# Feed-forward weight tiles split into two parts by GpSimd's casting and adding transfers

## The chip, the cores and the metric

The kernel runs on one core of a Trainium2 chip, as one launch. The metric is the device time of one execution in microseconds (us). A core has TensorE (matrix products, PE in the profile, with its weight loads as PEld), VectorE (DVE), ScalarE (ACT), GpSimd (POOL) and SyncE (SP, which here only issues transfers). Each engine works through its own queue in order, and waits on semaphores for the others.

## The reference

One layer of a diffusion backbone: 512 latent tokens and 256 context tokens, model width 1024, batch 1, all in float32. After the token mixers (a state-space scan and windowed attention) comes the part that matters here:

```python
def conv_ffn(h, w_up, conv_w, conv_b, w_down):
    u = dwconv_centred(h @ w_up, conv_w, conv_b)
    a, b = u[..., :D_FF], u[..., D_FF:]          # D_FF = 2816
    return (jax.nn.silu(a) * b) @ w_down
...
x = x + gt2 * conv_ffn(modulate(x, norm2_g[l], sh2, sc2), w_up[l], ffn_conv_w[l], ffn_conv_b[l], w_down[l])
...
return rmsnorm(x, final_g)
```

`sh2`, `sc2` and `gt2` are parts of `mod`, the product of the activated condition vector with `w_mod`.

## The kernel before

**Products in three passes.** TensorE multiplies in a shortened float format (float32r). To keep float32 accuracy every operand is split in two: `hi` is the value rounded to float32r, `lo` what is left over. A product is then hi x hi, hi x lo and lo x hi, accumulated in one PSUM bank. `gemm` (lines 190 to 201) does this for one weight tile: for each block of 128 x 128 weights, line 196 multiplies the weights' hi with the activations' hi, 197 with their lo, 199 the weights' lo with the activations' hi. So a tile's `lo` is first needed by its third matmul.

**Weight tiles.** A tile has 128 partitions by 1024 columns, eight blocks (512 KB). `load_raw` (143) has SP load it in float32 into a tile `wraw`, of which there are three buffers; `split` (151) has ScalarE write `hi` (a rounding copy, line 152) and VectorE write `lo` (a subtraction, line 153). `whi` and `wlo` have two buffers each, so two tiles are in use or being made, and up to three more lie in raw form. The same raw buffers carry the modulation weights: a key `("m", i)` is loaded and used raw, by VectorE's products with the condition vector in `m_step` (lines 739 to 759; 750, 752, 758 in the profile). `ELSEWHERE` gives a few tiles another place: `("up", 1)` goes to a corner of the feed-forward's result tiles `fh` and `fl` (`far_piece`, line 1851) that is not yet written.

**The order of work.** `run` (170) takes a list of steps, each with the keys of the tiles that it uses, and loads tiles in that order, a fixed number ahead of use. The instructions go through a scheduler that sets each engine's order; each engine then runs its own queue in order.

**The feed-forward stages.** `out_last` (1783) ends the output projection in two halves of 256 tokens, and starts the normalisation: sums of squares (line 239, TensorE), `ms` (249, VectorE), the inverse root `rs` (250, GpSimd), and a spread over partitions (256, TensorE). `norm2_k` (1812) makes the normalised activations `mh` and `ml`, block by block: `tb` (1815, VectorE), `mh` (1816, ScalarE), and `ml` by VectorE (1822) or, for odd blocks, GpSimd (1820). The first up step interleaves this with its products (1866). Steps 1 to 21 each use two tiles, `("up", t)` and `("up", 22 + t)`; between the products ScalarE and VectorE do the three-tap convolution, the gate, and the split of the result (1844 to 1849, and 1347 to 1349 for the first half). The remaining eight `m` steps are woven between the up steps. Then `down_step` (1894) makes seven output blocks from three tiles each (1024, 1024 and 768 columns), and `down_last` (1905) the eighth, the final normalisation and the stores. `close_c1` (1824) opens the pool `c2pool`, which holds `fh` and `fl`.

Of the kernel before, what the change touches and what calls it, by code (L numbers as in the profile page):

```python
# [10 lines left out]
F32R = mybir.dt.float32r  # L11
U8 = mybir.dt.uint8
AF = mybir.ActivationFunctionType
ALU = mybir.AluOpType
# [4 lines left out]
P = 128  # L19
# [5 lines left out]
NFF = 22  # L25
# [14 lines left out]
def raw(ap):  # L40
    return ap.bitcast(F32)
# [3 lines left out]
def tile_hybrid_layer(  # L45
# [31 lines left out]
    V, S, G, T = nc.vector, nc.scalar, nc.gpsimd, nc.tensor  # L77

    cpool = ctx.enter_context(tc.tile_pool(name="cpool", bufs=1))
    wpool = ctx.enter_context(tc.tile_pool(name="wpool", bufs=2))  # L80
# [37 lines left out]
    src = {}  # L118
# [24 lines left out]
    def load_raw(key):  # L143
        a, n = src[key]
        r = wpool.tile([P, 1024], F32, tag="raw", name="wraw", bufs=3)
        dma = nc.sync.dma_start(r[:, :n], a)
        if key[0] == "m":
            M_LOADS[key[1]] = dma
        return r, n

    def split(r, n, hi, lo):
        S.copy(hi[:, :n], r[:, :n])  # L152
        V.tensor_tensor(lo[:, :n], r[:, :n], raw(hi[:, :n]), ALU.subtract)  # L153

    ELSEWHERE = {}

    def load(key):
        r, n = load_raw(key)
        if key[0] == "m":
            return r  # L160
        if key in ELSEWHERE:
            hi, lo = ELSEWHERE[key]()
            split(r, n, hi, lo)
            return hi, lo
        hi = wpool.tile([P, 1024], F32R, tag="whi", name="whi", bufs=2)
        lo = wpool.tile([P, 1024], F32R, tag="wlo", name="wlo", bufs=2)
        split(r, n, hi, lo)
        return hi, lo

    def run(prog, early=None):  # L170

        seq = [k for keys, _ in prog for k in keys]
        have, nload, nuse = {}, 0, 0
        for keys, fn in prog:
            nuse += len(keys)
            while nload < min(nuse + 1 + (early in keys), len(seq)):
                have[seq[nload]] = load(seq[nload])
                nload += 1
            fn(*[have.pop(k) for k in keys])
# [102 lines left out]
    class Plan:  # L282
# [6 lines left out]
        def add(self, name, engine, cost, needs, rank, emit, whole=True, load=0.11, late=False):  # L289


            self.atoms[name] = dict(
                name=name, engine=engine, cost=cost, needs=needs, rank=rank, emit=emit, whole=whole, load=load,
                late=late, start=None,
            )
# [537 lines left out]
    Q, F = {}, {}  # L833
# [48 lines left out]
    q_split(first["q"], 0)  # L882
    k_step(0)[1](first["w"], first["r"])
    run([q_step(1), ([("v", i) for i in range(3)], v_step)])

    psum_pools(acc=(2, 1), score=(1, 2), pt=(3, 1), po=(1, 1))
# [724 lines left out]
    for g in range(4):  # L1611
# [6 lines left out]
        for c in range(4):  # L1618
# [4 lines left out]
            if c == 1 or g == 3:  # L1623
                prog += m[1 + c : 2 + c] if g == 3 else m[1:2]
        prog += s[9:10]
    run(prog)
    bpool.close()

# [44 lines left out]

    ELSEWHERE["os", 2] = lambda: tuple(yh[3][:, i : i + 2, :].rearrange("p a b -> p (a b)") for i in (0, 2))

# [82 lines left out]
    def piece_in(tag):  # L1758
        def fn():
            t = cp.tile([P, 2, 1024], F32R, tag=tag, name="wlast")  # L1760
            return t[:, 0, :], t[:, 1, :]

        return fn


    for o in (5, 6, 7):
        ELSEWHERE["out", o] = piece_in("yh%d" % (o - 5))

# [55 lines left out]
    def close_c1():  # L1824
        c1pool.close()
        c2pool = ctx.enter_context(tc.tile_pool(name="c2pool", bufs=1, reuse_waits="tile"))
        F["h"] = c2pool.tile([P, NFF, L], F32R, name="fh")
        F["l"] = c2pool.tile([P, NFF, L], F32R, name="fl")

# [24 lines left out]

    ELSEWHERE["up", 1] = far_piece

# [48 lines left out]
    def down_last(*w):  # L1905
# [52 lines left out]
        with tc.manual_schedule(engines={mybir.EngineType.PE}):  # L1958
# [6 lines left out]
            for f in (r["f"], finish(1)):  # L1965
                for _ in f:
                    pass

    run(
        [([], lambda: (y_split(range(8)), [square(True) for _ in range(4)], y_split(range(8, 12))))]  # L1970
        + fill[n3:]
# [3 lines left out]
        + weave([out_step(o) for o in range(5)], msteps[18:24])  # L1975
        + [([], vectors)]
        + [([("out", o) for o in (5, 6, 7)], out_last), ([], close_c1)]
        + weave([up_step(t) for t in range(NFF)], msteps[24:])
        + [down_step(o) for o in range(7)]
        + [([("dn", 21 + i) for i in range(3)], down_last)],  # L1980
        early=("g", 15),
# [85 lines left out]
```

## Time and profile before

| | |
|---|---|
| median of 2 runs | 1241.22 us (1241.05 and 1241.39) |
| span of the profiled execution, first to last instruction | 1239.5 us |
| TensorE busy | 1230.0 us, 99% |
| VectorE busy | 864.6 us, 70% |
| ScalarE busy | 656.3 us, 53% |
| GpSimd busy | 145.4 us, 12% |
| moved by transfers | 174.57 MB, 141 GB/s on average |

The page comes from one execution. Its own time is that of the span and the 1.6 to 1.9 us around it in the two runs. Engine rows give busy time and share of the span; matmuls overlap one another, so their durations add up to more than their pace. In a group, the name before the arrow is the tile that is written, the number after the bar the total busy time and the mean of one in ns, and the last field the idle time before and what ended it. A chain of waits goes back from the last instruction to what released each step. "To landing" is the time from the issue of a transfer to its completion.

### The profile page before, as it was taken

To read this page: it belongs to the slowest core of one execution; us is meant where nothing else is said; L and a number is where in the kernel's file an instruction comes from. 1 tells how busy PE (TensorE), PEld (TensorE's weight loads), DVE (VectorE), ACT (ScalarE), POOL (GpSimd) and SP (SyncE) were. 2 spreads that over 40 slices of the span, in tenths; PEclk is the share of its full clock that TensorE was granted. 3 is DMA by queue.
4 is the path that set the end of the run, shared out by engine and by line. 5 is a ranking of instruction groups with operands and counts; after the bars stand their busy time and mean duration, and the time that the engine had idled before them with its cause. 6 is when DMAs were issued, how large, how long until landed. Compare 5 with 4: busy or idle time off the path is not lost.

```text
span 1239.5 us, 17395 instructions
## 1 busy us (share of the span) xinstructions
PE 1230.0 (99%) x6464; PEld 1013.8 (82%) x6464; DVE 864.6 (70%) x1387; ACT 656.3 (53%) x1224; POOL 145.4 (12%) x145
## 2 busy tenths in 40 slices
PE   9999999999999999999999999999999999999997
PEld 6798888888888878777787788889888888888886
DVE  5857788888645697896987767576777767772333
ACT  5658788787454476475675653224544444442221
POOL 0000000000000052261542530000100000000000
PEclk9999999999999999999999999999999999999999
DMA  9643142222354336355365577674233333333331
GB/s 371 248 136 94 56 137 81 91 72 77 119 173 132 127 102 184 115 157 158 102 187 203 146 257 262 213 231 159 89 117 119 109 113 119 112 106 97 103 94 68
DMA packets 91189, 174.57 MB, mean 141 GB/s; under 512 B 7904, under 2 KB 43552, under 8 KB 91104
## 3 DMA queue, kind: packets, MB, share of 16 engines
q1 hardware_dynamic: 90128, 172.66, 43.9%
q8 instruction: 51, 0.84, 0.3%
q10 hardware_dynamic: 976, 0.79, 0.2%
q14 instruction: 34, 0.28, 0.1%
HBM read 150.82 MB, written 17.11 MB: 135 GB/s over the span
## 4 chain that ended last, share of the span: by engine, by line
PE 93%; DMA 3%; DVE 3%; ACT 1%; issue 0%; POOL 0%; DVEq 0%; SPq 0%; ACTq 0%; POOLq 0%
PE acc L196 21%; PE acc L199 21%; PE acc L197 21%; PE score L914 3%; PE po L963 3%; PE pt L950 2%; PE mis L536 2%; PE mis L1567 2%; PE mis L1460 2%; PE mis L1575 1%; DMA wraw<-wout 1%; PE acc L1033 1%; PE acc L1034 1%; PE acc L1035 1%; PE mis L1477 1%; PE mis L1375 1%
## 5 line engine op out<-in xcount | busy, mean ns | idle before, releaser
L153 DVE TENSOR_TENSOR wlo<-wraw,whi 128x1024 fp32r<-128x1024 f32 (+2 forms) x127 | 156.0, 1228 | 125.9 <-ACT whi L152 123.0
L152 ACT CAST whi<-wraw 128x1024 fp32r<-128x1024 f32 (+2 forms) x127 | 131.2, 1034 | 196.3 <-PE acc L197 142.5
L196 PE MATMUL acc<-hlh,whi 128*128 128x512 f32 x472 | 194.2, 411 | 0.0
L197 PE MATMUL acc<-hll,whi 128*128 128x512 f32 x472 | 185.0, 392 | 0.0
L199 PE MATMUL acc<-hlh,wlo 128*128 128x512 f32 x472 | 185.0, 392 | 0.0
L196 PE MATMUL acc<-mh,whi 128*128 128x512 f32 x368 | 143.4, 390 | 0.0
L197 PE MATMUL acc<-ml,whi 128*128 128x512 f32 x368 | 143.2, 389 | 0.0
L199 PE MATMUL acc<-mh,wlo 128*128 128x512 f32 x368 | 143.2, 389 | 0.0
L199 PEld LDWEIGHTS acc<-hlh,wlo 128*128 128x128 f32 x472 | 88.6, 188 | 19.5
L196 PEld LDWEIGHTS acc<-hlh,whi 128*128 128x128 f32 x472 | 88.8, 188 | 17.9 <-issue 3.1
L197 PEld LDWEIGHTS acc<-hll,whi 128*128 128x128 f32 x472 | 88.9, 188 | 17.4 <-issue 2.4
L1462 POOL TENSOR_TENSOR st<-st,eT 128x512 f32<-128x512 f32 x24 | 29.5, 1230 | 448.7 <-ACT st L1479 435.0
L197 PEld LDWEIGHTS acc<-ml,whi 128*128 128x128 f32 x368 | 69.1, 188 | 14.4
L196 PEld LDWEIGHTS acc<-mh,whi 128*128 128x128 f32 x368 | 69.1, 188 | 14.3
L199 PEld LDWEIGHTS acc<-mh,wlo 128*128 128x128 f32 x368 | 69.1, 188 | 14.2
L1348 DVE SCALAR_TENSOR_TENSOR ta<-acc,half,ta 128x511 f32<-128x511 f32 (+1 forms) x66 | 43.9, 665 | 27.3 <-ACT ta L1347 27.1
L923 DVE CUSTOM_DVE_ANT_0 p<-score,winm,nsink 128x512 f32<-128x512 f32 (+1 forms) x64 | 51.8, 810 | 15.3 <-PE score L914 13.8
L250 POOL TENSOR_TENSOR rs<-ms,phalf 128x2 f32<-128x2 f32 (+1 forms) x5 | 4.8, 956 | 475.2 <-DVE ms L249 475.2
L196 PE MATMUL acc<-fh,whi 128*128 128x512 f32 x154 | 60.0, 390 | 0.0
L197 PE MATMUL acc<-fl,whi 128*128 128x512 f32 x154 | 59.9, 389 | 0.0
L199 PE MATMUL acc<-fh,wlo 128*128 128x512 f32 x154 | 59.9, 389 | 0.0
L1347 ACT ACTIVATE ta<-acc,half 128x512 f32<-128x512 f32 (+1 forms) x66 | 46.9, 711 | 22.5 <-PE acc L199 21.2
(381 smaller groups left out, 2891.4 us busy)
## 6 DMA issues: line engine op xcount, KB each, us to landing
wraw<-wup SPq DMA_DIRECT2D x44, 512.0 KB, 3.4
fb<-cs_d SPq DMA_DIRECT2D x32, 512.0 KB, 6.2
wraw<-wm SPq DMA_DIRECT2D x32, 512.0 KB, 3.6
wraw<-wx SPq DMA_DIRECT2D x24, 512.0 KB, 3.6
wm<-wm SPq DMA_DIRECT2D x16, 512.0 KB, 8.4
wraw<-wz SPq DMA_DIRECT2D x16, 512.0 KB, 3.5
wraw<-wos SPq DMA_DIRECT2D x16, 512.0 KB, 4.8
wraw<-wdn SPq DMA_DIRECT2D x16, 512.0 KB, 3.5
```

What stands on the lines that cost most here:

```text
L152: S.copy(hi[:, :n], r[:, :n])
L153: V.tensor_tensor(lo[:, :n], r[:, :n], raw(hi[:, :n]), ALU.subtract)
L196: T.matmul(ps, wh, xh[:, k0 + k, :], start=a, stop=False)
L197: T.matmul(ps, wh, xl[:, k0 + k, :], start=False, stop=False)
L199: T.matmul(ps, wl, xh[:, k0 + k, :], start=False, stop=b)
L536: T.matmul(ps, w[a], h[b], start=c == 1, stop=c % n == 0, skip_group_check=True)
L914: T.matmul(ps[:, o : o + len(z) * P], Q[h][:, b * P : (b + 1) * P], k[:, j, z[0] * P : (z[-1] + 1) * P], start=v == 0 and o % 512 in (0, P ...
L923: V.tensor_tensor_reduce(p[:, :w], d["ps"][i][:, o0 : o0 + w], m, op0=ALU.add, op1=ALU.min, scale=1.0, scalar=nsink[:, h : h + 1], accum_o ...
L963: T.matmul(d["po"], vst[:, cols[x], j, :], d[y][x], start=x == 0 and y == "pth", stop=x == c - 1 and y == "ptl")
L1347: S.activation(o[:, :n], ps[:, :n], AF.Identity, scale=hcol(base_w, stride + i), bias=hcol(base_b, i))
L1348: V.scalar_tensor_tensor(o[:, 1:n], ps[:, 0 : n - 1], hcol(base_w, i), o[:, 1:n], ALU.mult, ALU.add)
L1462: G.tensor_tensor(h8(n), h8(s), bc64(eT[:, z0 : z0 + 8, c]), ALU.mult)
```

## The change

In place of load, rounding copy and subtraction, each tile of `w_up` and `w_down` except the first three used (`("up", 0)`, `("up", 22)`, `("up", 1)`) is made by a new function `load_split`: GpSimd issues a transfer from memory that casts into `hi`; ScalarE writes the negative of `hi` into `lo`; GpSimd issues a second transfer of the same weights that adds them into `lo`. No raw buffer is used. Two tiles of three use the buffers `whi` and `wlo`, the third a new pair `xhi` and `xlo` in `c2pool`, with one buffer each. In these stages tiles are asked for one further ahead.

```diff
+    THIRD = []
+
+    def load_split(key):
+
+        a, n = src[key]
+        THIRD.append(key)
+        if len(THIRD) % 3:
+            hi, lo = (wpool.tile([P, 1024], F32R, tag=t, name=t, bufs=2) for t in ("whi", "wlo"))
+        else:
+            hi, lo = (F["c2"].tile([P, 1024], F32R, tag=t, name=t, bufs=1) for t in ("xhi", "xlo"))
+        G.dma_start(hi[:, :n], a)
+        S.activation(lo[:, :n], raw(hi[:, :n]), AF.Copy, scale=-1.0)
+        G.dma_start(lo[:, :n], a, accum_op=ALU.add)
+        return hi, lo
 
     def load(key):
+        if key[0] in ("up", "dn") and key not in (("up", 0), ("up", 1), ("up", NFF)):
+            return load_split(key)
         r, n = load_raw(key)
...
         for keys, fn in prog:
             nuse += len(keys)
-            while nload < min(nuse + 1 + (early in keys), len(seq)):
+            more = keys and keys[0][0] in ("up", "dn")
+            while nload < min(nuse + 1 + (early in keys) + bool(more), len(seq)):
                 have[seq[nload]] = load(seq[nload])
...
         c2pool = ctx.enter_context(tc.tile_pool(name="c2pool", bufs=1, reuse_waits="tile"))
+        F["c2"] = c2pool
         F["h"] = c2pool.tile([P, NFF, L], F32R, name="fh")
```

## The prediction

> **What bounds the kernel now.** I read the page first: engine totals, slices and the chain that ended last.
>
> ```profile
> span 1239.5 us, 17395 instructions
> PE   1230.0 (99%) x6464; PEld 1013.8 (82%) x6464; DVE 864.6 (70%) x1387; ACT 656.3 (53%) x1224; POOL 145.4 (12%) x145
> PEclk9999999999999999999999999999999999999999
> PE 93%; DMA 3%; DVE 3%; ACT 1%; issue 0%; POOL 0%; DVEq 0%; SPq 0%; ACTq 0%; POOLq 0%
> ```
>
> TensorE holds the chain. That is an average, so next comes the view of busy time by stretches, cut at the feed-forward stages: the first up step with its normalisation, the other up steps, the down products, the tail.
>
> ```profile
> core 0: us, PE busy (x) PEld busy (x) DVE busy (x) ACT busy (x) POOL busy (x), PEclk, DMA share, GB/s
> 866.00:878.40 12.40, 12.40 (x102) 12.02 (x102) 7.89 (x17) 7.74 (x18) 5.92 (x7) 1.00 0.14 44
> 878.40:1112.00 233.60, 233.60 (x1036) 193.46 (x1036) 170.09 (x216) 101.75 (x131) 0.00 (x0) 1.00 0.35 113
> 1112.00:1228.00 116.00, 116.00 (x574) 98.58 (x573) 35.01 (x38) 27.43 (x33) 0.70 (x1) 1.00 0.27 81
> 1228.00:1239.50 11.50, 3.51 (x27) 2.98 (x26) 6.33 (x17) 0.88 (x3) 2.11 (x3) 0.78 0.52 182
> ```
>
> From 878.4 to 1228 TensorE is never idle. Matmul durations overlap (389 ns each below), so I take the pace from the chain in order of time: three matmuls, one weight block, from one L197 to the next.
>
> ```profile
> 882.15 0.23 PE acc L197
> 882.83 0.23 PE acc L197
> ```
>
> That is 0.68 us a block, 0.227 a matmul: **5.44 us for a tile of eight blocks**, 4.08 for the 768-wide tiles of the down product. The groups by line of 880 to 1120 us show what the split costs other engines, and beside it the modulation products:
>
> ```profile
> L196 PE MATMUL acc<-mh,whi 128*128 128x512 f32 x328 | 127.7, 389 | 0.0
> L153 DVE TENSOR_TENSOR wlo<-wraw,whi 128x1024 fp32r<-128x1024 f32 x44 | 53.9, 1224 | 34.5 <-ACT whi L152 34.5
> L152 ACT CAST whi<-wraw 128x1024 fp32r<-128x1024 f32 x44 | 46.3, 1055 | 27.2 <-PE acc L197 27.2
> L1848 ACT CAST fh<-ta 128x512 fp32r<-128x512 f32 x22 | 13.7, 621 | 59.3 <-DVE ta L1847 59.3
> L752 DVE SCALAR_TENSOR_TENSOR tm<-wraw,csil,tm 128x512 f32<-128x512 f32 x14 | 10.5, 747 | 0.4 <-DMA wraw<-wm 0.2
> L758 DVE TENSOR_REDUCE mod<-mis 128x4 f32<-128x512 f32 x2 | 1.4, 692 | 1.8 <-PE mis L756 1.8
> L750 DVE TENSOR_SCALAR tm<-wraw,csil 128x512 f32<-128x512 f32 x2 | 1.0, 480 | 0.1
> ```
>
> **What the change removes is worth nothing.** The two programs' orders of instructions show 65 tiles changed (the short description says 63): 41 of wup, 24 of wdn. VectorE loses 65 subtractions, about 65 x 1.224 = 80 us; ScalarE swaps a cast for a negating copy of the same size, 1.05 us; SP loses 65 loads. No TensorE idle time stands against any of these between 878.4 and 1228, so I credit 0; the cover is TensorE itself, which has no gap to give back.
>
> **What it adds is a serial chain on one queue.** GpSimd now issues 130 transfers. Before, a raw tile waited in its own buffer and only cast and subtraction (2.3 us) followed once an operand buffer was free. Now the load itself goes into that buffer, so it starts only when TensorE has finished the tile there; then come negation, the second transfer, and only then the tile's third matmul (0.45 us in). In the up steps GpSimd's order repeats by three (tiles counted from the first changed one):
>
> ```
> xhi 6 (after TensorE ends 3)  wlo 5  xlo 6  whi 7  wlo 7  whi 8  xhi 9 (after TensorE ends 6)  wlo 8 ...
> ```
>
> Each `lo` waits for ScalarE, and everything behind it waits too: whi 8 cannot be issued until wlo 7 has been, though its buffer is free. This is the wait that I expect last.
>
> No transfer of this sort is in the trace. The nearest rows are SP's plain transfers of the same 512 KB, the spread of the weight loads (last line, issue to landing), and GpSimd's shortest and longest instruction nearby:
>
> ```profile
> wraw<-wup SPq DMA_DIRECT2D x44, 512.0 KB, 3.4
> fb<-cs_d SPq DMA_DIRECT2D x32, 512.0 KB, 6.2
> wraw<-wm SPq DMA_DIRECT2D x32, 512.0 KB, 3.6
> wm<-wm SPq DMA_DIRECT2D x16, 512.0 KB, 8.4
> DMA to landing us min/median/max: 2.9/3.4/4.8
> 857.94 0.70 POOL L250 TENSOR_TENSOR rs<-ms,phalf 128x2 f32<-128x2 f32 x1 [112.61 <-DVE ms L249]
> 867.93 1.65 POOL L250 TENSOR_TENSOR rs<-ms,phalf 128x2 f32<-128x2 f32 x1 [1.32 <-DVE ms L249]
> ```
>
> - First transfer, issue to landing, H: 3.4 to 8.4. I take 4.8, the slowest weight load, since two transfers will often be in flight.
> - Adding transfer, Q: 3.4 to 16.8 (two of the 8.4). It reads the weights and the destination, so I take two plain loads, 6.8, near the 6.2 row.
> - GpSimd's own time per transfer, g: 0.70 to 1.65; I take the middle, 1.2.
> - Negation with its place in ScalarE's queue, A: 1.05 to 4.4. The fh cast ahead of it waits 59.3/22 = 2.7 and runs 0.62; half of that added gives 2.7.
>
> The Trainium skill (DMA: Bandwidth & Descriptors, Bandwidth and the fitted cost in "Anatomy of one DMA") gives a GpSimd-issued transfer as 2.0 us plus bytes over 436 GB/s; by that both H and Q would be an estimated 3.2 us, and the sum below 1256 us. Against it, the same skill (Collectives: The Full Stack, "Why ReduceScatter is half of AllGather") has an add in the transfer at half the rate (62.28 against 32.35 GB/s) because it reads two sources: Q would be twice my H, 9.6, and the sum 1371. No run here shows either yet.
>
> *Up steps.* From the end of tile 3 to the start of tile 8: H+A+g for tile 6, H+A+g for 7, H+A+Q for 8, less 0.45: 14.4 + 8.1 + 2.4 + 6.8 - 0.45 = 31.25. Tiles 8 and 9 then take 10.88: 42.1 for six tiles that need 32.64 now. That is 4.75 lost per three tiles; 13 such groups: **62 us**.
>
> *Down products.* The three tiles of one output run 14.96 us. Order: xhi, xlo, whi, whi, wlo, wlo. From the end of one x tile to the start of the next output's second tile: H+A+g+H+A+Q-0.45, where A is 1.7 (only a square of some 0.63 stands ahead) = 20.55, so 5.6 late. A late start also moves the point from which the next chain counts, so the lateness alternates between 5.6 and nothing: 2.8 on average. Eight outputs: **22 us**.
>
> *The first changed tile.* Today its raw data lies ready when the first up step ends at 878.4. Now both its transfers start then, while TensorE has one tile (5.44) to run: H+A+Q-0.45-5.44 = **8.4 us**.
>
> *The modulation products move.* With the raw buffers free, SP loads all eight remaining wm tiles early, and the new order on VectorE puts their 16 products (and two reductions) into the normalisation before and inside the first up step.
>
> ```profile
> 849.82 1.23 DVE L153 TENSOR_TENSOR wlo<-wraw,whi 128x1024 fp32r<-128x1024 f32 x1 [0.17 <-ACT whi L152]
> 857.71 0.16 DVE L249 TENSOR_SCALAR ms<-mis 128x2 f32<-128x2 f32 x1 [2.91 <-PE mis L239]
> 860.54 0.87 DVE L1815 SCALAR_TENSOR_TENSOR tb<-x,a,mis 128x256 f32<-128x256 f32 x2 [1.53 <-PE mis L256]
> 872.86 0.48 DVE L1822 SCALAR_TENSOR_TENSOR ml<-tb,mod,mh 128x256 fp32r<-128x256 f32 x1 [0.25 <-ACT mh L1816]
> ```
>
> The first wm tile is loaded when the buffer of 849.82+1.23 comes free: 851.05 + 3.6 = 854.7; its products end at 855.9; the third reuses that buffer, lands at 859.5, and its product ends at 860.2. The ms of 857.71 stands behind it: 2.5 us late, and TensorE waits for what follows from ms. Inside the second half another reduction, a small addition (0.16, the size of ms) and products (0.69 + 0.16 + 0.48 + 3 x 0.75 = 3.6) enter a chain that has about 0.25 us of slack at each of four pairs, so 2.6 remain. Together **5 us**, from 2.5 (second part hidden) to 10 (xhi 3 at 8.4 instead of 4.8 also holds ScalarE, whose negation of it stands ahead of the last of the first half's activations).
>
> *Sum.* The two runs' median, 1241.22, is 1.7 above the profiled span; all terms lie inside the span. 1239.5 + 1.7 + 62 + 22 + 8.4 + 5 = **1339 us**. With the low ends everywhere (H and Q 3.4, g 0.7, A 1.05) the up chain is 17.7 + 10.88 = 28.6 against 32.64: no stall there, 2 for the first tile, 2.5 to 5 for the products: 1247. With H and Q 8.4, g 1.65, A 2.7 it is 11.4 per up group and 7.4 per output: 148 + 59 + 14 + 10, 1472; with Q at 16.8 about 1570. No bound lies below 1241, as there is no idle TensorE time to win.
>
> **Rivals.**
>
> *The transfers land like SP's.* Then the third buffer covers the chain: 1247 as above. For it: 3.4 us at 0.35 DMA share, so the engines are far from full. Against: 3H+Q must stay within 32.64 - 10.88 + 0.45 - 3A - 2g, which is 17.7 us at the low A and g but 11.7 at mine, with an addition among the transfers. So it decides from about 3 to 4.4 us a landing, by ScalarE's queue. This is the case that is not slower.
>
> *The DMA engines become the bound.* One tile per 5.44 us is 96 GB/s, by the 0.35 at 113 GB/s a share of 0.30. Plain first transfer and two-read addition make 0.9, just below the limit; if casting costs two units and adding three, it is 1.5, and the 343 us of TensorE time for the 65 tiles (57 x 5.44 + 8 x 4.08) become 515: 1241 + 172 + 13 = 1426. Against it: source and destination have four bytes alike.
>
> *The stalls slow TensorE's clock.* The last stretch above, where TensorE is mostly waiting, has a granted clock of 0.78. If the feed-forward ran at that, 343 us become 440, 97 more: 1436. Against it: between my stalls lie two to three whole tiles of work, and the clock is 1.00 in every other stretch. The Trainium skill (TensorE: Matmul & The Clock Gate, Part 1) has half clock after an idle window of about 3.4 us; the 0.78 agrees in kind, and only stalls longer than mine on average would bring it.
>
> **How the numbers follow.** Forecast 0.53; DMA engines 0.20; clock 0.11; landings like SP's 0.14; 0.02 for a gain that I cannot see. Range: 1260 leaves out most of the case of landings like SP's, and 1540 takes in both slow rivals and nearly the slow bound, so that some 2 in 10 lie outside. The forecast's own range is 1285 to 1420. Over 2% (25 us, about what a measurement of this kernel tells from no change): slower 0.86, within 0.12 (the SP-like case, with a little over the limit), faster 0.02.
>
> **What would show it.** Right: TensorE idle before L199 (the lo matmul) by some 4 us in every three tiles, released by transfers into wlo and xlo; the adding transfer landing in about 7 us against 5 for the first; VectorE about 80 us less busy; DMA share near 0.9 in the up steps; ms near 860. Wrong: TensorE still without a gap after 878 (landings short); share at 1 with landings beyond 10 us (engines); a clock below 1 between 890 and 1200 (clock); or a wait on GpSimd's issue time itself.

## The result, and the profile after

The changed kernel takes **1341.24 us** (runs of 1344.72 and 1337.75) against 1241.22: a ratio of 1.081, interval 1.074 to 1.087. The forecast was 1339. The profiled execution is the one of 1344.72, with a span of 1342.9, 103.4 more than before. Four lines of its page answer to those shown of before: span, engines, TensorE's granted clock by slices, and the chain that ended last.

```profile
span 1342.9 us, 17410 instructions
PE 1261.5 (94%) x6464; PEld 1028.2 (77%) x6464; DVE 791.3 (59%) x1322; ACT 655.5 (49%) x1224; POOL 240.1 (18%) x275
PEclk9999999999999999999999999979989998999989
PE 59%; issue 32%; POOL 6%; DMA 2%; DVE 1%; ACT 0%; POOLq 0%; DVEq 0%; ACTq 0%
```

VectorE has 73 us less to do, and nothing came of it. TensorE fell from 93% to 59% of the chain; "issue" is time in which GpSimd's queue stood without anything that the chain can name. Of its 423 us, 115 are one piece from 745.55 us on, ahead of the changed tiles, where TensorE was busy; most of the rest is GpSimd behind ScalarE, which waits for a transfer. The clock row, whole before, has dents in the last third. The busy time by stretches, cut at the end of the first up step, at TensorE's first matmul on a transferred `lo`, at the first down matmul and at the end of the seventh output (`down_last` makes the eighth):

```profile
core 0: us, PE busy (x) PEld busy (x) DVE busy (x) ACT busy (x) POOL busy (x), PEclk, DMA share, GB/s
889.40:900.20 10.80, 5.28 (x25) 3.65 (x24) 8.69 (x14) 5.79 (x8) 2.89 (x4) 0.88 0.66 157
900.20:1177.40 277.20, 238.91 (x980) 190.24 (x981) 101.44 (x140) 94.23 (x120) 55.91 (x79) 0.96 0.68 151
1177.40:1314.60 137.20, 114.59 (x464) 90.25 (x463) 10.85 (x15) 25.00 (x31) 29.88 (x42) 0.95 0.68 147
```

TensorE, which had no gap, is idle for 38.3 us of the up steps and 22.6 of the down products. The transfer engines are at a share of 0.68, so they are not full. The waits from 850 us on (total, times, longest) say at which instruction:

```profile
POOL wlo L168 <- ACT wlo L167: 169.3, 42, 9.1
ACT wlo L167 <- DMA whi<-wup: 93.1, 27, 5.2
PE acc L216 <- DMA wlo<-wup: 42.9, 21, 4.6
PE acc L216 <- DMA wlo<-wdn: 13.9, 7, 2.7
```

Read from the bottom: TensorE (line 216, the matmul on `lo`) waits for the adding transfer; that stands on GpSimd behind ScalarE's negation (167); and the negation waits for the casting transfer. One turn of GpSimd's queue shows the order (start, duration, and in brackets the idle time before it and its releaser; 166 is the casting transfer, 168 the adding one):

```profile
1045.88 0.55 POOL L166 DMA_DIRECT2D whi<-wup  x1
1055.57 0.85 POOL L168 DMA_DIRECT2D wlo<-wup  x1 [9.14 <-ACT wlo L167]
1056.12 0.86 POOL L166 DMA_DIRECT2D whi<-wup  x1
1059.41 0.54 POOL L166 DMA_DIRECT2D xhi<-wup  x1 [2.43 <-PE acc L216]
1063.73 0.87 POOL L168 DMA_DIRECT2D wlo<-wup  x1 [3.78 <-ACT wlo L167]
```

It is the order of the prediction, whi 7, wlo 7, whi 8, xhi 9, wlo 8, and the wait expected last is the longest: for 9.14 us `wlo` waits and the next `whi` stands behind it. That is the longest of 42 such waits, which are 4.0 us on average (169.3/42). Over the stretch from 900.2 a tile takes 277.2/40.9 = 6.78 us, 20.3 for three, against 16.3 before. Of these 4.0 us TensorE waits 2.8 (three times 38.3/40.9); the rest is matmuls that run slower, of which more below.

### The profile page after: what moved, and what is told of

The parts are those of the page before. It is cut to its first block, busy times and chain, and to the rows that moved or that the text cites. A ratio compares the mean times of both kernels' runs of the same rounds, so it can differ in the third digit from the quotient of the medians.

```text
span 1342.9 us, 17410 instructions
## 1 busy us (share of the span) xinstructions
PE 1261.5 (94%) x6464; PEld 1028.2 (77%) x6464; DVE 791.3 (59%) x1322; ACT 655.5 (49%) x1224; POOL 240.1 (18%) x275
## 4 chain that ended last, share of the span: by engine, by line
PE 59%; issue 32%; POOL 6%; DMA 2%; DVE 1%; ACT 0%; POOLq 0%; DVEq 0%; ACTq 0%
PE acc L216 11%; PE acc L213 11%; PE acc L214 11%; PE score L931 3%; PE po L980 3%; PE pt L967 2%; PE mis L553 2%; PE mis L1584 2%; POOL whi L166 2%; POOL wlo L168 2%; PE mis L1477 2%; DMA wlo<-wup 2%; PE mis L1592 1%; PE acc L1050 1%; PE acc L1052 1%
## 5 line engine op out<-in xcount | busy, mean ns | idle before, releaser
L216 PE MATMUL acc<-mh,wlo 128*128 128x512 f32 x264 | 109.8, 416 | 42.9 <-DMA wlo<-wup 42.9
L167 ACT ACTIVATE wlo<-whi 128x1024 fp32r<-128x1024 f32 (+1 forms) x44 | 44.9, 1020 | 152.2 <-DMA whi<-wup 93.1
L152 ACT CAST whi<-wraw 128x1024 fp32r<-128x1024 f32 (+2 forms) x62 | 64.6, 1041 | 93.4 <-PE acc L214 57.1
L213 PE MATMUL acc<-mh,whi 128*128 128x512 f32 x264 | 107.3, 407 | 0.9 <-DVE tm L769 0.7
L214 PE MATMUL acc<-ml,whi 128*128 128x512 f32 x264 | 106.8, 404 | 0.0
L153 DVE TENSOR_TENSOR wlo<-wraw,whi 128x1024 fp32r<-128x1024 f32 (+2 forms) x62 | 78.5, 1267 | 36.5 <-ACT whi L152 34.3
L216 PEld LDWEIGHTS acc<-mh,wlo 128*128 128x128 f32 x264 | 52.2, 198 | 62.4 <-DMA wlo<-wup 51.7
L1863 DVE SCALAR_TENSOR_TENSOR tc<-acc,vec,tc 128x511 f32<-128x511 f32 x22 | 16.5, 750 | 87.7 <-ACT tc L1862 87.7
L213 PEld LDWEIGHTS acc<-mh,whi 128*128 128x128 f32 x264 | 52.4, 198 | 12.0 <-ACT tb L1855 1.1
L214 PEld LDWEIGHTS acc<-ml,whi 128*128 128x128 f32 x264 | 52.1, 197 | 11.5
L947 ACT ACTIVATE p<-p,mneg 128x512 f32<-128x512 f32 (+1 forms) x64 | 49.7, 777 | 15.4 <-DVE mneg L940 14.8
```

The lines of the kernel that those rows point to most:

```text
L167: S.activation(lo[:, :n], raw(hi[:, :n]), AF.Copy, scale=-1.0)
L213: T.matmul(ps, wh, xh[:, k0 + k, :], start=a, stop=False)
L214: T.matmul(ps, wh, xl[:, k0 + k, :], start=False, stop=False)
L216: T.matmul(ps, wl, xh[:, k0 + k, :], start=False, stop=b)
L947: S.activation(p, p, AF.Exp, bias=d["mneg"][:, i : i + 1], scale=-1.0, accum_out=d["den"][:, i : i + 1])
```

## The experiments

Each is a small edit of the changed kernel. Beside each time stands its ratio to the kernel before on the same chip (1240.4 to 1240.6), with the interval.

### A fourth pair of buffers

```diff
+        if len(THIRD) % 4 == 0:
+            hi, lo = (wpool.tile([P, 1024], F32R, tag="raw", name=t, bufs=3) for t in ("rhi", "rlo"))
-        if len(THIRD) % 3:
+        elif len(THIRD) % 4 != 3:
...
-            while nload < min(nuse + 1 + (early in keys) + bool(more), len(seq)):
+            while nload < min(nuse + 1 + (early in keys) + 2 * bool(more), len(seq)):
```

> A fourth pair of operand buffers (in the raw buffers that the changed tiles no longer use), and loads started one tile further ahead; transfers, bytes and arithmetic as in the changed kernel. Serial chain on GpSimd's queue (my theory): a buffer is given back one whole tile (5.44 us) earlier than it is needed, more than the 4.0 us that a group of three now loses (52 us over 13 groups), so most of the 52 us of the up steps and some 20 of the 31 us of the down products go: 1265 to 1285 us; TensorE's waits for wlo and xlo fall below 20 us, and the half-clock stretches (51 us in twelve) below 15 us. Transfer engines (share 0.68 now): the same bytes take the same time, 1335 to 1345. Clock as a cause of its own: stalls shorter, but the half-clock stretches stay, 1310 to 1325.

Measured: **1298.98 us**, 1.048 (1.046 to 1.050). The chain was held by its buffers in part: 42 us come back, not the 56 to 76 expected. Some 5 of them are not the chain's: the fourth pair takes the raw buffers, the modulation products come later, and TensorE is through the tile after the first up step (its last matmul on `fl`) at 887.51 and not 892.44. The view by stretches, and the landings (count, size, median from issue to landing), show what took the rest:

```profile
889.40:1139.40 250.00, 233.27 (x989) 189.21 (x989) 110.51 (x156) 91.39 (x120) 55.51 (x78) 0.97 0.76 180
```

```profile
rlo<-wup POOLq DMA_DIRECT2D x9, 512.0 KB, 7.8
```

With more transfers in flight the share is 0.76 and the fourth pair's adding transfer lands in 7.8 us, where 5.5 was usual. A chain that is given room fills it partly with slower landings.

### The low part last

```diff
+        if late:
+            for k in range(nk):
+                wh = hi[:, k * m : (k + 1) * m]
+                for ps, xh, xl in targets:
+                    T.matmul(ps, wh, xh[:, k0 + k, :], start=first and k == 0, stop=False)
+                    T.matmul(ps, wh, xl[:, k0 + k, :], start=False, stop=False)
+            for k in range(nk):
+                for ps, xh, xl in targets:
+                    T.matmul(ps, lo[:, k * m : (k + 1) * m], xh[:, k0 + k, :], start=False, stop=last and k == nk - 1)
+            return
```

> In the up steps after the first and in the down products, a tile's sixteen matmuls on the high part run first and the eight on the low part last; no transfer is changed. The low part is then needed 3.6 us into the tile and not 0.45, and the high buffer comes free 1.8 us before the tile's end. Serial chain: up to 5 us more per turn of a buffer against 4.0 lost in a group of three up tiles, so the up steps' 52 us fall to 0 to 10 and the down products' 31 to 5 to 15: 1265 to 1285 us. Transfer engines: nothing changes, 1335 to 1345. Clock: where the stalls fall below 1 us, the half-clock stretches must go with them; if these stay, 1310 to 1325.

Measured: **1312.79 us**, 1.058 (1.054 to 1.061): 28 us back, half of the least that was expected. A row of the landings view carries the reason that I can show:

```profile
xhi<-wup POOLq DMA_DIRECT2D x12, 512.0 KB, 6.8
```

The casting transfer into `xhi`, 4.1 us in the changed kernel, takes 6.8, as the earlier release lets it run beside an adding one. That the order on GpSimd changed too is seen; its share was not measured.

### A plain second transfer

```diff
-        G.dma_start(lo[:, :n], a, accum_op=ALU.add)
+        G.dma_start(lo[:, :n], a)
```

> The second transfer casts the weights into the low buffer without adding (the addition of the negated high part is left out; every wait, issue and buffer stays). It measures what the addition costs. If the addition's reading of the destination is what makes 5.0 to 5.6 us of it, the landing falls to the 3.4 to 4.8 us of a plain one, 0.7 to 2.1 us per chain of three: 1310 to 1333 us. If a second transfer in flight makes it, the landing stays at 5 to 6 us and the time at 1335 to 1343. If the transfer engines were the bound, less traffic would show at once: share from 0.68 towards 0.45, and the time below 1300.

The addition is left out: `lo` then holds the weights and not what is left over. Measured: **1272.55 us**, 1.026 (1.022 to 1.029). 69 us of 100 hang on the addition, far more than the 8 to 31 expected, and the time lies where I had put the engines as the bound; the runs after this one separate that. The landings of the changed kernel, then of this one:

```profile
whi<-wup POOLq DMA_DIRECT2D x28, 512.0 KB, 6.2
wlo<-wup POOLq DMA_DIRECT2D x28, 512.0 KB, 5.5
xhi<-wup POOLq DMA_DIRECT2D x12, 512.0 KB, 4.1
```

```profile
whi<-wup POOLq DMA_DIRECT2D x28, 512.0 KB, 4.6
wlo<-wup POOLq DMA_DIRECT2D x28, 512.0 KB, 3.9
xhi<-wup POOLq DMA_DIRECT2D x13, 512.0 KB, 3.8
```

`whi` and `wlo` fall by 1.6 us: without the addition the second transfer itself is shorter, and so is the casting one that is issued 0.55 us behind it, which the edit did not touch. `xhi`, issued later, falls by only 0.3. An addition is therefore paid several times in the chain: two landings of `whi`, one of `xhi` and one adding landing lie in the chain of six tiles, and 3 x 1.6 + 0.3 is 5.1 of the 8.0 us that six tiles lose. That is about the part of the time, 69 of 100 us, that came back.

### The same, with bytes that nobody waits for

```diff
+        r, n = load_raw(key)
         G.dma_start(hi[:, :n], a)
-        S.activation(lo[:, :n], raw(hi[:, :n]), AF.Copy, scale=-1.0)
-        G.dma_start(lo[:, :n], a, accum_op=ALU.add)
+        S.activation(lo[:, :n], raw(hi[:, :n]), AF.Identity, scale=-1.0, bias=r[:, 0:1])
+        G.dma_start(lo[:, :n], a)
```

> As the run with a plain second transfer (the addition of the negated high part is left out), plus one plain 512 KB load on SP's queue for each tile into a raw buffer that ScalarE's negation reads one column of; it lands ahead of time and adds no wait to the chain, only bytes for the DMA engines: three reads' worth for each tile. If bytes in flight make the landings long, they go from 4.6 and 3.8 back to 5.5 and more, and the time from 1273 to 1310 to 1345 us. If it is the addition itself, landings rise by less than 0.6 us and the time stays at 1272 to 1292.

The addition is left out here too; each tile has a plain load more, of which the negation reads one column. Measured: **1319.78 us**, 1.064 (1.062 to 1.066): 47 of the 69 us are lost again, by transfers that add no step to the chain. The chains lost more than that: as the loads take the raw buffers, the modulation products come later, and the last matmul on `fl` starts at 882.86, 9 us earlier than with a plain second transfer alone (892.00).

```profile
whi<-wup POOLq DMA_DIRECT2D x26, 512.0 KB, 5.6
wlo<-wup POOLq DMA_DIRECT2D x28, 512.0 KB, 4.7
```

The landings rose by 1.0 and 0.8 us; the upper one reaches what was expected of load on the engines, the other stays short of it. So more than half of what the addition cost can be had by bytes in flight alone; whether the addition costs something beyond its bytes stays open.

### One transfer per tile

```diff
-        G.dma_start(hi[:, :n], a)
+        r, n = load_raw(key)
+        S.copy(hi[:, :n], r[:, :n])
```

> The first transfer goes back to SP's queue as a plain load into a raw buffer, ahead of time, and ScalarE casts it into the high part; the negation and the adding transfer on GpSimd stay. The DMA engines move the same bytes for each tile. Serial chain: a buffer's turn is now cast 1.05 + negation 1.05 + GpSimd 0.9 + adding landing 5.5 = 8.5 us, inside the two tiles (10.88 us) of cover, and no casting transfer stands behind a waiting one: 1250 to 1275 us, TensorE's waits for the low parts below 20 us. Load on the DMA engines (share 0.68 at the changed kernel's pace, 0.85 at full pace): the adding landings go above 7 us and the time stays above 1300.

Measured: **1250.65 us**, 1.008 (1.006 to 1.010). This is the run that tells chain and engines apart: the same bytes and the same addition for each tile, but SP loads the tile ahead and ScalarE casts it, so that the casting transfer is out of the chain and out of GpSimd's queue. Of the 91 us that come back, some 6 are the modulation products', which the raw buffers now hold back (the last matmul on `fl` starts at 886.85, not 892.44). The rows are of the stretches of up steps and down products, TensorE's waits, and the landings.

```profile
892.20:1118.90 226.70, 225.95 (x987) 186.77 (x988) 112.05 (x156) 132.55 (x161) 34.58 (x40) 0.98 0.85 201
1118.90:1223.80 104.90, 104.90 (x466) 86.84 (x465) 11.70 (x17) 46.22 (x53) 18.20 (x21) 1.00 0.85 182
```

```profile
PE acc L217 <- DMA wlo<-wup: 4.8, 1, 4.8
```

```profile
wlo<-wup POOLq DMA_DIRECT2D x28, 512.0 KB, 5.5
```

At a share of 0.85, where the changed kernel has 0.68, TensorE has no gap in the down products and one wait in the up steps, for the first changed tile. The adding landing is 5.5 as before and harms nobody. In these runs the engines' load costs time only through the length of a chain that has no slack.

### The modulation products kept late

```diff
-                    V.tensor_scalar_mul(acc, r[:, 0:512], sc)
+                    one = V.tensor_scalar_mul(acc, r[:, 0:512], sc)
...
+                if i >= 24:
+                    tc.keep_in_program_order(one)
```

> The products of the last eight modulation tiles are kept out of the second normalisation on VectorE: they stand behind the up steps' work as in the program's order. The feed-forward's transfers are as in the changed kernel. If the moved products make the late ms and the waits in the first up step (9.6 us lost between 849 and 889 in the changed kernel's profile), 6 to 10 us come back: 1331 to 1336 us. If the delay there comes from ScalarE's and GpSimd's new order, 1340 to 1343.

Measured: **1327.87 us**, 1.069 (1.064 to 1.075), 13 us back and a little more than expected; its interval and the changed kernel's touch. VectorE's order shows the cause, first in the changed kernel, then here:

```profile
859.27 1.53 DVE L769 SCALAR_TENSOR_TENSOR tm<-wraw,csil,tm 128x512 f32<-128x512 f32 x2
860.72 0.15 DVE L266 TENSOR_SCALAR ms<-mis 128x2 f32<-128x2 f32 x1
```

```profile
856.79 0.16 DVE L266 TENSOR_SCALAR ms<-mis 128x2 f32<-128x2 f32 x1 [2.91 <-PE mis L256]
```

The products stood directly in front of `ms`. Without them the first up step ends at 877.3 instead of 889.3, and the last matmul on `fl`, in the tile after it, starts at 882.46 instead of 892.44: 10 us. The four runs lie between 1317.8 and 1333.4, so the 13 us are not finer than that.

### The first three changed tiles as before

```diff
-        if key[0] in ("up", "dn") and key not in (("up", 0), ("up", 1), ("up", NFF)):
+        if key[0] in ("up", "dn") and key not in (("up", 0), ("up", 1), ("up", 2), ("up", NFF), ("up", NFF + 1), ("up", NFF + 2)):
```

> The changed kernel, but the first three changed tiles are loaded and split as before the change; that also takes their raw buffers, so the modulation products stay out of the normalisation by themselves. It takes away the two small terms of the sum (5 us for the products, 8.4 for the first tile) and leaves the chains (62 and 22 us, less one group of three). If those terms stand at what the changed kernel's profile shows (9.6 and 6.6 us), 1318 to 1328 us. If the lost time only moves to the next tiles, 1333 to 1343.

Measured: **1326.91 us**, 1.070 (1.068 to 1.071). The time is in the range, but only one of the two terms went; that the number fits is luck in part. The first up step ends at 877.9 and not 889.3; the first tile's wait moved:

```profile
894.37 0.60 POOL L166 DMA_DIRECT2D whi<-wup  x1 [17.00 <-PE acc L216]
908.09 0.79 PE L216 MATMUL acc<-mh,wlo 128*128 128x512 f32 x1 [5.65 <-DMA wlo<-wup]
```

The old tiles hold both `whi` buffers, so the first casting transfer starts at 894.37 and TensorE waits 5.65 us (and 1.58 for `whi`) three tiles later. Wherever the new chain begins, it begins uncovered.

### Only the down products

```diff
-        if key[0] in ("up", "dn") and key not in (("up", 0), ("up", 1), ("up", NFF)):
+        if key[0] == "dn":
```

> Only the 24 tiles of the down products are made by the two GpSimd transfers; the up steps are as before the change. The sum has the down products as a term of its own, 22 us; the changed kernel's stage is 32.4 us longer than before. If their chain stands by itself: 1262 to 1275 us, the down stage 125 to 138 us against 104.9, and the up steps unchanged. If it comes from what the up steps leave behind (late buffers, late transfers), the down stage stays below 115 and the time below 1253.

Measured: **1272.74 us**, 1.026 (1.024 to 1.028).

```profile
877.60:1107.00 229.40, 229.40 (x1018) 190.05 (x1017) 164.86 (x209) 100.36 (x129) 0.65 (x2) 1.00 0.33 108
1107.00:1241.30 134.30, 114.37 (x465) 90.56 (x464) 11.49 (x17) 25.01 (x30) 29.74 (x42) 0.95 0.69 153
```

The up steps are what they were, and the down products lose 29.4 us by themselves (134.3 against 104.9). The loss is their own chain's, not left over from the up steps.

### The remedies together

Four buffers, low part last, and late modulation products (the three diffs above):

> Fourth pair of buffers, low part last, and the modulation products kept out of the normalisation, together; both transfers of each tile as in the changed kernel. One by one they took 42, 28 and 13 us off. If the chain's length against its cover is all, they add up, since each gives a turn more room: 1250 to 1265 us. If each transfer takes longer the more of them are in flight (in the fourth-buffer run the fourth pair's adding transfer landed in 7.8 us against 5.5, and the DMA share rose from 0.68 to 0.76), the gains do not add: 1270 to 1290 us, with adding landings of 6 to 8 us and casting ones near 7.

Measured: **1313.96 us**, 1.060 (1.058 to 1.061), which is worse than the fourth pair alone. Two reductions of modulation products hold TensorE for 19.3 us (the longer wait is 11.5). Their tiles share three raw buffers with the fourth pair. The next run leaves that remedy out:

> Fourth pair of buffers and low part last, without the third remedy: the modulation products may move again. With all three the time was 1314, where two reductions of modulation products held TensorE for 19 us (their tiles share three raw buffers with the fourth pair). If that sharing is what undid the gain, this gives 1270 to 1290 us, below the 1299 of the fourth pair alone, with no long wait for those reductions. If more transfers in flight are what undid it (casting landings 6.8 there against 6.2), it stays at 1299 to 1320.

Measured: **1324.60 us**, 1.068 (1.066 to 1.070). TensorE's wait for the reductions is gone and the time is worse, so that wait is not what undid the gain. The sharing itself is still there: `rhi` waits for VectorE's modulation products, 24.8 us in seven waits (18.6 with the fourth pair alone). One turn of GpSimd's queue (four tiles; 168 casts, 170 adds):

```profile
1029.66 0.89 POOL L168 DMA_DIRECT2D whi<-wup  x1
1033.99 0.55 POOL L168 DMA_DIRECT2D rhi<-wup  x1 [3.44 <-DVE tm L781]
...
1040.15 0.87 POOL L168 DMA_DIRECT2D whi<-wup  x1
1047.90 0.87 POOL L170 DMA_DIRECT2D wlo<-wup  x1 [6.87 <-ACT wlo L169]
1048.45 0.87 POOL L168 DMA_DIRECT2D xhi<-wup  x1
1056.15 0.86 POOL L170 DMA_DIRECT2D xlo<-wup  x1 [6.83 <-ACT xlo L169]
...
1058.16 0.88 POOL L168 DMA_DIRECT2D whi<-wup  x1
```

Two of the four casting transfers are followed at once by their own tile's adding one, which waits 6.8 us for them while nothing else can be issued: 28.5 us for four tiles that TensorE needs 21.8 for. The free buffers can't be used, because the queue that would fill them is waiting. What TensorE waits for in these up steps is mostly no weight tile:

```profile
PE acc L215 <- issue: 32.5, 13, 3.5
```

```profile
1031.15 0.77 PE L215 MATMUL acc<-mh,xhi 128*128 128x512 f32 x1 [3.15 <-issue]
```

All 13 waits stand at the first matmul of a tile, which opens a new accumulator (a PSUM bank); from 888 us to the end of the up steps TensorE idles 34.5 us in all. Each of the 13 ends 0.10 us after VectorE's last read of an older accumulator (here 1030.30 + 0.75). VectorE comes late because ScalarE's part of that read (1376, at 1028.72) stood behind two negations, the first of which had waited 6.22 us for its casting transfer. So a casting transfer that lands late holds TensorE by a second way, through ScalarE's queue and the accumulator. That the bank is what releases TensorE is read from these times; the view names no releaser, and no run tests it. With all three remedies the same row has 16.4 us in five waits; in the changed kernel it is absent.

The three remedies with a plain second transfer:

> The three remedies together and a plain second transfer (the addition is left out). With landings of 3.8 to 4.6 us and room for 8 us and more per turn, the chain hides wholly: 1241 to 1250 us, what is left being the first changed tile. If it is above 1255, something besides the chain and the landings costs time (GpSimd's or ScalarE's queue, or the clock).

Measured: **1253.45 us**, 1.011 (1.009 to 1.013), between the two expectations. TensorE has one group of waits left between 850 and 1240 us, 8.7 us in two waits for the reductions of the modulation products as above; beside it, short landings leave next to nothing of the loss.

### The best version

One transfer per tile, the first three changed tiles as before, and late modulation products:

> The run with one transfer per tile on GpSimd, and also: the first three changed tiles are loaded and split as before the change, so that the next tiles' chains start under their 16 us, and the modulation products stay out of the normalisation. That run stood 10 us above the kernel before: 8.2 of it between the first up step and the end of the up steps, 3 in the normalisation, none in the down products. Serial chain: both go, 1240 to 1244 us, level with the kernel before and not below it, as TensorE then never waits although VectorE has some 75 us less to do. Load on the DMA engines (0.86 in that run's up steps): something over 5 us stays, 1246 to 1252.

Measured: **1249.11 us**, 1.007 (1.006 to 1.009). The number lies where the load on the engines was expected to leave it, but the trace does not show that cause:

```profile
902.60 0.80 PE L217 MATMUL acc<-mh,wlo 128*128 128x512 f32 x1 [2.57 <-DMA wlo<-wup]
912.74 0.50 PE L217 MATMUL acc<-mh,wlo 128*128 128x512 f32 x1 [1.78 <-DMA wlo<-wup]
```

```profile
914.00:1113.00 199.00, 199.00 (x881) 164.72 (x880) 100.20 (x140) 118.85 (x144) 31.04 (x36) 1.00 0.89 206
```

From 914 TensorE is busy without a gap at a share of 0.89. The loss sits at two early `wlo` tiles, where the chain starts, as in the changed kernel with its first tiles as before. My expectation that three tiles would cover the start was wrong. What the waits leave of the 8.6 us is mostly slow matmuls behind the first of them. No version beat the kernel before: TensorE is full there, and relief for VectorE has nothing to free.

## Why the prediction was right, step by step

The forecast held because the chain that it describes is what TensorE waits for. That the number came out within 3 us is luck: two pairs of errors cancelled, and the waits, which were all that was forecast, were too few by 26 us, while matmuls that ran slowly, put at nothing, made that up. The terms against the profile, by TensorE's matmuls: the stages after 849 us end at 889.3, 1177.5 and 1314.8 (first up step, last up step, seventh output), before at 878.2, 1107.7 and 1212.5. Ten matmuls of the next tile, 2.3 us, moved forward into the first. The last column is what TensorE's waits (idle time by the views above) make of each.

| term | predicted | measured | of it waits |
|---|---|---|---|
| modulation products in the normalisation | 5 | 40.3 - 29.2 - 2.3 = 8.8 | 4.8 - 0.3 = 4.5 |
| first changed tile | 8.4 | 10.80 - 5.28 = 5.5 of waits (stretch from 889.4), 1.7 of slow matmuls behind them: 7.2 | 5.5 |
| up steps | 62 | 288.2 + 2.3 - 229.5 - 7.2 = 53.8 | 38.3 |
| down products (seven of eight outputs) | 22 | 137.3 - 104.9 = 32.4 | 22.6 |
| sum | 97.4 | 102.2 of 103.4 | 70.9 |

**The chain.** Right as to place, order and wait: TensorE idles before the `lo` matmul, though 2.8 us in three tiles where 4.75 was forecast; with the slow matmuls behind the waits 4.0 are lost. Its terms were mis-sized in opposite directions. H was taken as 4.8 and is 6.2 for `whi` and 4.1 for `xhi`; Q was taken as 6.8 and is 5.5. 3H + Q is 22.0 where the sum had 21.2. The sign "about 7 us against 5 for the first" came the other way round, as the adding transfer lands sooner than the casting one beside it. The error was to treat the addition as a price of the adding transfer; the plain-second run shows it shared out over the casting transfers beside it. g was 1.2 and is 0.54 to 0.88. A was 2.7; in the turn shown, GpSimd's adding issue starts 1.35 us after the negation does (1054.22 to 1055.57):

```profile
1054.22 1.06 ACT L167 ACTIVATE wlo<-whi 128x1024 fp32r<-128x1024 f32 x1 [4.73 <-DMA whi<-wup]
1066.30 1.04 ACT L167 ACTIVATE xlo<-xhi 128x1024 fp32r<-128x1024 f32 x1
```

ScalarE's queue, which I put into A, seldom stands in front of `whi`: 27 of the 28 negations of `whi` in the up steps waited for the casting transfer (the row of waits above). It can stand in front of `xhi`: the second row has no wait, and starts 2.5 us after its transfer (issued at 1059.41, 4.4 us to landing) had landed. With A at 1.35 throughout the chain is 16.5 + 4.05 + 1.7 + 5.5 - 0.45 = 27.3, and 38.2 with the two tiles, against 40.6 measured for six; an estimate, as A is from one turn. The 2.4 that are missing are of the size of what it leaves out, `xhi`'s place in ScalarE's queue and slow matmuls in the two tiles; no run separates these.

**The down products.** Here a step failed: that "the lateness alternates between 5.6 and nothing". The additions to the residual end each output; before they came every 14.96 us.

```profile
1196.07 0.75 DVE L1918 SCALAR_TENSOR_TENSOR x<-acc,mod,x 128x512 f32<-128x512 f32 x1 [13.91 <-PE acc L216]
...
1314.96 0.75 DVE L1918 SCALAR_TENSOR_TENSOR x<-acc,mod,x 128x512 f32<-128x512 f32 x1 [15.70 <-PE acc L216]
```

Seven rows, six intervals: 19.8 us each, so 4.9 late on average where 2.8 was taken. No output is on time, as every second one was to be: the six are late by 6.0, 4.2, 5.2, 2.4, 5.5 and 5.9. TensorE's waits are 3.2 us an output (22.6/7); the rest is slow matmuls. Why the lateness does not alternate, no run shows.

**The modulation products.** `ms` at 860.72, predicted 860.2. The term was under-sized, 8.8 and not 5, though its waits were 4.5; the rest is slow matmuls again (granted clock 0.85 from 866.0 to 889.4). Keeping the products late gave 13 us back, from runs that scatter by 16.

**The rivals.** *Landings like SP's* (1247): casting transfers of 512 KB do land in 3.6 us at the least (one of `xhi`), but `whi`, mostly issued right behind an adding one, takes 6.2. The sum that the prediction calls "below 1256 us" is 1256.5 by its own terms, and falls with it. *The engines as the bound* (1426): the share of 0.9 that the prediction worked out for full pace is there in the runs with one transfer per tile, 0.85 to 0.89, and TensorE doesn't wait; what was wrong in my list of signs is that the changed kernel itself would show it, since it runs too slowly for that and shows 0.68. The engines matter through landings: 47 us and more came from bytes alone. *The clock slowed by stalls* (1436) was partly real, and the forecast's sum had nothing for it:

```profile
900.19 0.79 PE L216 MATMUL acc<-mh,wlo 128*128 128x512 f32 x1 [4.60 <-DMA wlo<-wup]
900.78 0.63 PE L213 MATMUL acc<-mh,whi 128*128 128x512 f32 x1
901.21 0.63 PE L214 MATMUL acc<-ml,whi 128*128 128x512 f32 x1
```

After some stalls matmuls start every 0.43 us instead of 0.227. In the up steps and down products that is so behind ten of the 19 waits of 2 us or more and behind none of the shorter ones; most of these stretches last 2.6 to 3.4 us. With a granted clock of 0.96 and 0.95 in the two stages that is an estimated 11 + 7 = 18 of the 102 us, inside the stage lengths of the table; the rival had 0.78 throughout. Part of the slow work lies in the cover of the chain, where TensorE would have waited instead, so what a full clock would have saved stays open. The clock follows the stalls: from 914 in the best version there are none, and the clock is 1.00. The Trainium skill (TensorE: Matmul & The Clock Gate, Part 1) has half clock after an idle window of about 3.4 us, with a window that runs freely. The length agrees in part, 3.4 us in four of the ten stretches; but a stall of 2.57 us was followed by one too (902.60 above) and one of 1.78 wasn't, so a stall shorter than a window can be enough.

The Trainium skill's two-source reading of additions (Collectives: The Full Stack, "Why ReduceScatter is half of AllGather"), by which the prediction had a sum of 1371, is half borne out. GpSimd's queue takes 15.8% of 1251.5 us for 65 adding transfers in the one-transfer run, 3.04 us of all engines for each, and 16.6% of 1274.0 us for 130 plain ones in the plain-second run, 1.63:

```profile
q0 software_dynamic: 9360, 33.03, 15.8%
```

```profile
q0 software_dynamic: 18720, 66.07, 16.6%
```

That is 1.87 times the work of the engines, near the page's two. The landing is only 5.5 against 3.9, 1.4 times, so the sum of 1371, which took 9.6 for it, was too high.

## What to carry to other kernels

Before work is moved from a compute engine to transfers, write out the whole turn of a buffer, landings included, in the order of the queue that issues them: with a wait for another engine between two transfers, everything behind it stands still, on the engine that waits too, and more buffers help only in part (42 of 100 us here). Landing times are not constants; take them from rows with as many transfers in flight as the changed kernel will have. Relief for an engine that was not the bound was worth nothing here, while the new waits of the one that was full came on top of its time, and made it slower behind them.

## What the runs showed of the hardware that was not expected

- An adding transfer slowed its neighbour as much as itself: 1.6 us for the casting transfer of 512 KB issued right behind it (6.2 against 4.6), 1.6 us for its own landing (5.5 against 3.9).
- A load that nobody waits for lengthened others' landings by 0.8 to 1.0 us at a share of only 0.71, while a share of 0.89 cost nothing where the chain had slack. In these runs the share did not tell whether transfers cost time.
- Some versions whose TensorE stalls scatter, 1317.8 to 1333.4 in the four runs with late modulation products, where the kernel before has 1240.1 to 1241.5 in seven; others do not, 1326.6 to 1328.2 with the first changed tiles as before.
- A wait of 2.57 us was enough for some 2.6 us of matmuls at about half pace behind it; a wait of 1.78 us had none.
